# A fp32 Fourier/Hyena encoder layer: the weight parts of the first gate tiles are no longer held behind ScalarE's last row copy of the Fourier stage

## Chip, cores and metric
One core of a Trainium2 chip runs the whole program in one launch. The metric is device time in microseconds (us), the median of several runs. Two numbers of one profiled execution are used beside it: its own time, and the span that the profiler recorded. Engines are named as in the profile: PE (TensorE matmul), DVE (VectorE), ACT (ScalarE), POOL (GpSimd) and SP (the engine that issues most loads and stores).

## What is computed
Two sequences of 1024 rows and 1024 channels go through one encoder layer in float32. Cut to what matters here:

```
p = rmsnorm(x) @ w_in                      # fv, fg, hv (3 parts), hg, mg (2 parts)
fz = fftn(fv as 4 groups of 256, axes=(sequence, channel)).real
y_f = (fz * silu(fg)) @ w_fourier_out      # Fourier branch
kf = rfft(two implicit filters per channel, each normalised by its sum of magnitudes)
z = v; z = x1 * long_conv(z, kf[0]); z = x2 * long_conv(z, kf[1])   # Hyena branch
y_h = (z * silu(hg)) @ w_hyena_out
out = (sigmoid(mg_f) * y_f + sigmoid(mg_h) * y_h) @ w_out;  x + rmsnorm(out)
```

## The kernel before
**Numbers.** Every float32 operand is split into a high part h and a rest l, and a product is three matmuls (h·h, l·h, h·l), all recorded by one helper (L194). A split is a ScalarE copy to h (L171) and a DVE subtraction for l (L181).

**Stages.** `_body` (L1487) runs the set-up, `phase_fourier` (L489), `phase_main` (L901) and `phase_blocks` (the output projections). There is one instruction list for the whole program. Tile pools carry the buffers and their waits, and a scheduler that runs its own simulation of the engines' timelines when the program is built chooses in which order each engine gets its instructions; the order of the Python code is only its starting point. Within an engine that order is fixed: an instruction that waits holds everything behind it. `issue_after(ins)` puts in one more rule for that scheduler: what is made under it must stand behind `ins` on its engine.

**Fourier stage.** `fourier_half` (L386) runs four times, twice for each sequence. Near its end, for each of two channel groups g, it makes the odd part of the sequence transform (`pse`, `pso`, from tiles `oo`), turns it into `qp`, and for two column parts n multiplies by the channel tables into `pP` and `pQ`. ScalarE copies `pP` out twice (L475 into `fPs`, L476 scaled into `fPm`); DVE combines them with `pQ` into rows `fA` and `fB` (L480 to L485), and POOL issues the two stores to `d_fz` (L486, L487). In the kernel before, the name `self.rows` keeps the instruction of L476 that was made last: the last row copy of the last half.

**Main stage.** `load_x` loads the normalised input as eight parts, each split into `xh` and `xl` (128x1024; SP load, ScalarE cast, DVE subtraction). Then come 16 filters. `filter_taps` (L619) builds one filter's taps: `pft` matmuls, exponentials `ex` on ScalarE, taps `T` and a sum of magnitudes on DVE, two small `pn` matmuls (L652, L653) and a reciprocal on DVE (L654), which occurs once a filter and so marks the 16 steps in a trace. `filter_spectrum` (L660) transforms the taps (`pXf` matmuls, DVE before and after). The taps of filter i+1 are made ahead of the spectrum of filter i, and with the last filter the first two convolutions' projections are made as well.

**Gate tiles.** To give PE work beside the filters, 30 gate tiles (8 each of sections 0, 5 and 6 of `w_in`, 6 of section 4) are spread evenly over the 16 filters: one or two behind each, the first filter gets one. A gate tile (`spill_gate`, L793) calls `inproj` (L739), which takes the 128x1024 weight tile in two halves. A half needs: a place for its h and l (`rooms`: tags wh/wl with two buffers, then one tile `whl` in either of two more pools, in turn), an SP load into `wr` (two buffers, L757), a ScalarE copy to h (L762), a ScalarE multiplication that writes -h into l (L763), and a POOL-issued DMA that adds the weight from memory onto l (L764). Then 24 matmuls follow; with both halves a tile has 48 matmuls of 512 columns, 24 into each of two `pin` outputs of one PSUM bank (tag mm has four banks). ScalarE copies them out (L802, or Silu at L806 with a DVE product by `fz`), and SP stores them.

**What the change touches.** While the tile of the first filter is made, `self.opening` is true, and L762 and L763 stand under `issue_after(self.rows.ins)`: both ScalarE steps of that tile come behind the last row copy. The second tile has no rule of its own, but its `wr` loads need the buffers that the first tile's copies read.

After the filters, `branches` runs the convolutions of both sequences with further projections beside them.

Of the kernel before, what the change touches and what calls it, by code (L numbers as in the profile page):

```python
# [12 lines left out]
AF = mybir.ActivationFunctionType  # L13
# [148 lines left out]
class K:  # L162
# [223 lines left out]
    def fourier_half(self, b, half, W, fo, px, pf, begun={}):  # L386

        nc = self.nc
        WE, WO = W

        def pair(shape, tag, bufs=1):
            return [pf.tile(shape, F32R, tag=f"{tag}{i}", name=f"{tag}{i}", bufs=bufs) for i in range(2)]
# [54 lines left out]
        vec = self.vec  # L447
# [6 lines left out]
        for g in range(2):  # L454
            Pp, Qp = PP[g], pair([P, 514], "qp")
            co = slice(P * g, P * g + P)
            stage(P, lambda m: (OO[0][:, m, co], OO[1][:, m, co]), 1, None, Qp, "XT"[g])
            A = pf.tile([P, 1026], F32, tag="fA", name="fA", bufs=1)
            B = pf.tile([P, 1026], F32, tag="fB", name="fB", bufs=1)
            gg = 2 * half + g  # L460
            for n in range(2):
                w = (258, 256)[n]
                ns = slice(258 * n, 258 * n + w)
                pr, qr = (Pp[0][:, ns], Pp[1][:, ns]), (Qp[0][:, ns], Qp[1][:, ns])
                pP = self.psum("X", 2, "pP")[:, :w]
                self.mm3(pP, (ch[:, 0, 0:P], ch[:, 1, 0:P]), pr, True, False)
                self.mm(pP, cx[:, 0, g, :], PX[:, ns], False, True)
                pQ = self.psum("X", 2, "pQ")[:, :w]
                self.mm3(pQ, (ch[:, 0, P:2 * P], ch[:, 1, P:2 * P]), qr, True, False)
                self.mm(pQ, ch[:, 0, 2 * P:3 * P], pr[0], False, False)  # L470
                self.mm(pQ, ch[:, 0, 2 * P:3 * P], pr[1], False, False)
                self.mm(pQ, cx[:, 1, g, :], PX[:, ns], False, True)
                Ps = pf.tile([P, 258], F32, tag="fPs", name="fPs", bufs=2)
                Pm = pf.tile([P, 258], F32, tag="fPm", name="fPm", bufs=1)
                nc.scalar.copy(Ps[:, :w], pP)  # L475
                self.rows = nc.scalar.activation(Pm[:, :w], pP, AF.Copy, scale=vec[:, 11:12])  # L476
                t0 = 258 * n
                w = (258, 255)[n]
                r = slice(0, w)
                self.stt("dve", A[:, t0:t0 + w], pQ[:, r], vec[:, 10:11], Ps[:, r])  # L480
                self.add("dve", B[:, t0:t0 + w], pQ[:, r], Pm[:, r])
                w = (258, 254)[n]
                r = slice(0, w)
                self.stt("dve", A[:, 1024 - t0:1024 - t0 - w:-1], pQ[:, r], vec[:, 11:12], Ps[:, r])
                self.stt("dve", B[:, 1024 - t0:1024 - t0 - w:-1], pQ[:, r], vec[:, 12:13], Pm[:, r])  # L485
            nc.gpsimd.dma_start(self.d_fz[b][2 * gg], A[:, 0:1024])  # L486
            nc.gpsimd.dma_start(self.d_fz[b][2 * gg + 1], B[:, 0:1024])  # L487
# [251 lines left out]
    def inproj(self, sec, mt, b=None, plain=False):  # L739

        nc, a = self.nc, self.a
        ps = [self.psum("mm", 4, f"pin{n}") for n in range(2)]
        for q in range(2):
            s = slice(512 * q, 512 * q + 512)
            src = a["w_in"][sec, mt][:, s]
            kept = self.d_w[sec - 1][mt] if b is not None else None
            if b or plain:
                h, l = [self.wp.tile([P, 512], F32R, tag=g, name=g, bufs=2) for g in ("wh", "wl")]
            else:
                h, l = self.rooms()  # L750
            if b:
                self.keep_parts()
                for t, k in zip((h, l), kept):
                    nc.sync.dma_start(t.bitcast(F32), k[:, s])
            else:
                r = self.wp.tile([P, 512], F32, tag="w", name="wr", bufs=2)
                nc.sync.dma_start(r, src)  # L757
                if plain:
                    self.split(h, l, r, "dve", "act")
                else:  # L760
                    with self.tc.issue_after(self.rows.ins) if self.opening else ExitStack():
                        nc.scalar.copy(h, r)  # L762
                        nc.scalar.mul(l, h, -1.0)  # L763
                    nc.gpsimd.dma_start(l, src, accum_op=ADD)  # L764
                    self.keep_parts()
                    if kept:
                        self.unsaved = [(t, k[:, s]) for t, k in zip((h, l), kept)]
            h, l = [t.rearrange("p (a b) -> p a b", a=4) for t in (h, l)]
            for n in range(2):
                for kk in range(4):  # L770
                    k = 4 * q + kk
                    s = slice(512 * n, 512 * n + 512)
                    self.mm3(ps[n], (h[:, kk], l[:, kk]), (self.xh[k][:, s], self.xl[k][:, s]), k == 0, k == 7)
        return ps
# [126 lines left out]
    def phase_main(self, nct=8, nb=NB, nf=16):  # L901
        tc, nc, a = self.tc, self.nc, self.a
        with ExitStack() as es:
            pool = lambda n: es.enter_context(tc.tile_pool(name=n, bufs=1, reuse_waits="tile"))
            mf, wa, wb, mi = pool("mf"), pool("wa"), pool("wb"), pool("mi")
            self.stage2 = pool("m2")
            self.turn, self.unsaved = 3, []
            ws = Rooms(wa, wb)
            self.load_x(0, range(4))
            self.hid = ws.tile([P, L], F32R, tag="q", name="hid", bufs=2)  # L910
            hid = ws.tile([P, L], F32, tag="q", name="hidr", bufs=2)
            nc.sync.dma_start(hid, self.d_h)
            nc.scalar.copy(self.hid, hid)
            self.sub("dve", self.hid[64:128], hid[64:128], self.hid[64:128])
            taps = self.filter_taps(0, 0, ws)
            self.load_x(0, range(4, 8))
            self.cfw0 = mf.tile([P, 4 * P], F32, name="cfw0")
            self.cfwd = mf.tile([P, 2, 12 * P], F32R, name="cfwd")
            nc.sync.dma_start(self.cfw0, a["c_fw0"])
            nc.gpsimd.tensor_copy(self.cfwd[:, 0, 0:1], self.xl[4][:, 0:1])  # L920
            nc.gpsimd.dma_start(self.cfwd, a["c_fwd"])
            for t, n in ((self.th, "c_th"), (self.wsh, "w_short"), (self.bm, "b_merge")):
                nc.sync.dma_start(t, a[n])
            plain = [(5, c) for c in range(8)] + [(6, c) for c in range(8)] + [(4, c) for c in range(NH)]
            fill = sorted([((2 * c + 1) / len(plain), t) for c, t in enumerate(plain)]
                          + [((2 * c + 1) / max(NF, 1), (0, c)) for c in range(NF)])
            fill = [t for _, t in fill]
            for i in range(nf):
                nxt = self.filter_taps((i + 1) % 2, (i + 1) // 2, ws) if i + 1 < nf else None
                if i == nf - 1:  # L930
                    first = [self.conv(1 + n, 0, ws, "vx"[n], 0, True) for n in range(2)]
                self.filter_spectrum(i % 2, i // 2, taps, ws)
                taps = nxt
                self.opening = i == 0
                for sec, c in fill[i * len(fill) // nf:(i + 1) * len(fill) // nf]:
                    self.spill_gate(0, sec, c, ws)
                if i == min(2, nf - 1):
                    self.cinv = mi.tile([P, 2, INVW], F32R, name="cinv")
                    nc.gpsimd.dma_start(self.cinv, a["c_inv"])
            self.branches(nb, nct, ws, *first)  # L940
# [575 lines left out]
```

## Time and profile before

| | us |
|---|---|
| median of 3 runs | 2438.34 (2437.77 to 2440.07) |
| profiled execution, its own time | 2444.92 |
| profiled execution, its span | 2443.1 |
| PE busy, share of span | 2371.6 (97%) |
| DVE busy | 1986.3 (81%) |
| ACT busy | 1177.0 (48%) |
| POOL busy | 449.3 (18%) |

The granted TensorE clock over the span is 0.99 of full speed. The profiled execution took 6.58 us more than the median of the runs. A start time in a timeline is counted in us from the span's start; "x3" means three instructions put together in one row, the duration then being that of all; what stands in square brackets is how long the engine had waited before the row, and for whom. A view by windows gives, for each stretch of time, its length, the busy time of each engine with its number of instructions, the clock that was granted to PE (1.00 is full), and what the DMA engines did.

### The profile page before, as it was taken

The page shows a single profiled execution, that of the slowest core. Times are in us where ns is not written, and L with a number is a line of the kernel's source. Part 1 is how long each engine was busy: PE and PEld are TensorE (multiplying, and loading weights), DVE is VectorE, ACT ScalarE, POOL GpSimd, SP SyncE. Part 2 cuts the span into 40 slices and gives each one's busy share as a digit, 9 for nine tenths or more (in the row PEclk, how much of TensorE's full clock was granted, in tenths as well). Part 3 has the DMA queues.
Part 4 walks back from the last instruction along what each step waited for, and adds up shares of the span by engine and source line. Part 5 has one row for each costly group of instructions (what it writes and reads, how often), then busy time and mean ns, then how long its engine had stood idle before and what let it go on. Part 6 is the DMA issues. An engine that isn't in the chain of part 4 may idle for free. (4 is left out here: it accounts for less than half of the span.)

```text
span 2443.1 us, 37244 instructions
## 1 busy us (share of the span) xinstructions
PE 2371.6 (97%) x13006; PEld 2058.6 (84%) x13006; DVE 1986.3 (81%) x3840; ACT 1177.0 (48%) x2220; POOL 449.3 (18%) x568
## 2 busy tenths in 40 slices
PE   5998899999999999999999999999999999999998
PEld 4987788888888888888888888888888888888786
DVE  7687777777776899899899999998667687778777
ACT  5545677776754444343332322333334375656543
POOL 1331111111122232321124444310000000101000
PEclk9998899999999999999999999999999999999999
DMA  8544876777777767665455666553646687978744
GB/s 319 171 160 173 239 198 193 202 203 198 214 213 236 203 201 203 190 180 167 172 181 181 217 208 214 190 172 135 215 147 216 213 306 248 279 263 228 224 155 155
DMA packets 262980, 499.65 MB, mean 205 GB/s; under 512 B 26550, under 2 KB 90263, under 8 KB 262408
## 3 DMA queue, kind: packets, MB, share of 16 engines
q1 hardware_dynamic: 220076, 380.53, 46.7%
q0 software_dynamic: 42528, 116.72, 18.3%
q8 instruction: 102, 1.67, 0.3%
q14 instruction: 86, 0.70, 0.1%
q10 hardware_dynamic: 188, 0.02, 0.0%
HBM read 333.59 MB, written 167.77 MB: 205 GB/s over the span
## 5 line engine op out<-in xcount | busy, mean ns | idle before, releaser
L194 PE MATMUL pin<-xh,wl 128*128 128x512 f32 x1024 | 401.7, 394 | 3.0 <-DMA wl<-in_w_in 2.4
L194 PE MATMUL pin<-xh,wh 128*128 128x512 f32 x1024 | 403.2, 394 | 0.9 <-ACT wh L762 0.9
L194 PE MATMUL pin<-xl,wh 128*128 128x512 f32 x1024 | 402.8, 393 | 0.0
L194 PE MATMUL pin<-xh,whl 128*128 128x512 f32 x896 | 292.4, 396 | 0.0
L194 PEld LDWEIGHTS pin<-xh,wl 128*128 128x128 f32 x1024 | 193.8, 189 | 38.8 <-DMA wl<-in_w_in 2.6
L194 PEld LDWEIGHTS pin<-xh,wh 128*128 128x128 f32 x1024 | 194.0, 190 | 36.1 <-ACT wh L762 1.2
L194 PEld LDWEIGHTS pin<-xl,wh 128*128 128x128 f32 x1024 | 193.9, 189 | 35.0
L194 PEld LDWEIGHTS pin<-xh,whl 128*128 128x128 f32 x896 | 167.7, 189 | 32.5
L194 PE MATMUL pT<-cinv,yh 128*128 128x256 f32 x1024 | 192.8, 283 | 2.3 <-ACT yh L171 2.3
L194 PE MATMUL pin<-xl,whl 128*128 128x512 f32 x448 | 177.7, 397 | 0.0
L194 PEld LDWEIGHTS pT<-cinv,yh 128*128 128x128 f32 x1024 | 165.5, 191 | 12.4 <-ACT yh L171 2.7
L194 PE MATMUL pX<-bh,cfwd 128*128 128x256 f32 x768 | 159.5, 288 | 1.1 <-ACT bh L171 1.1
L181 DVE TENSOR_TENSOR t<-pX,k 128x1024 f32<-128x1024 f32 x128 | 156.1, 1219 | 4.0 <-PE pX L194 3.1
L171 ACT CAST yh<-y 128x512 fp32r<-128x512 f32 x128 | 79.3, 620 | 158.1 <-DVE y L181 120.4
L194 PE MATMUL pT<-cinv,yl 128*128 128x256 f32 x512 | 145.6, 284 | 0.0
L171 ACT CAST bh<-b 128x512 fp32r<-128x512 f32 x144 | 88.9, 619 | 105.9 <-DVE b L181 69.6
L194 PEld LDWEIGHTS pX<-bh,cfwd 128*128 128x128 f32 x768 | 126.1, 192 | 4.8 <-ACT bh L171 1.6
L181 POOL TENSOR_TENSOR draw<-draw 128x256 f32<-128x256 f32 x96 | 92.4, 963 | 114.8 <-DMA draw<-in_w_out 39.8
L181 DVE TENSOR_TENSOR bl<-b,bh 128x512 fp32r<-128x512 f32 x144 | 101.3, 706 | 12.0 <-ACT bh L171 11.9
L194 PE MATMUL pX<-bl,cfwd 128*128 128x256 f32 x384 | 109.7, 286 | 0.0
L181 DVE TENSOR_TENSOR yl<-y,yh 128x512 fp32r<-128x512 f32 x128 | 90.6, 708 | 16.4 <-ACT yh L171 16.2
L194 PEld LDWEIGHTS pT<-cinv,yl 128*128 128x128 f32 x512 | 98.2, 192 | 1.9
(366 smaller groups left out, 6091.9 us busy)
## 6 DMA issues: line engine op xcount, KB each, us to landing
k<-d_k SPq DMA_DIRECT2D x128, 512.0 KB, 4.4
wr<-in_w_in SPq DMA_DIRECT2D x136, 256.0 KB, 3.5
d_g<-gt SPq DMA_DIRECT2D x92, 256.0 KB, 3.5
d_k<-kt SPq DMA_DIRECT2D x128, 128.0 KB, 2.8
d_k<-kt SPq DMA_DIRECT2D x64, 256.0 KB, 2.5
fz<-d_g SPq DMA_DIRECT2D x64, 256.0 KB, 5.5
wl<-in_w_in POOLq DMA_DIRECT2D x56, 256.0 KB, 5.2
whl<-in_w_in POOLq DMA_DIRECT2D x56, 256.0 KB, 5.4
```

The lines of the kernel that those rows point to most:

```text
L171: self.rounded = nc.scalar.copy(h, src)
L181: return e.tensor_tensor(out, a, b, op=op)
L194: return self.nc.tensor.matmul(out, lhsT, rhs, start=start, stop=stop, skip_group_check=shared)
```

## The change
Three places are edited. The last row copy's instruction is no longer kept, the ScalarE steps of the first filter's gate tile no longer stand under `issue_after`, and the flag that told them apart is gone. The instructions themselves are the same; the scheduler is free to put them elsewhere. In the changed kernel line numbers from L762 on are lower by one, from L935 on by two.

```
@@ -473,7 +473,7 @@
                 Ps = pf.tile([P, 258], F32, tag="fPs", name="fPs", bufs=2)
                 Pm = pf.tile([P, 258], F32, tag="fPm", name="fPm", bufs=1)
                 nc.scalar.copy(Ps[:, :w], pP)
-                self.rows = nc.scalar.activation(Pm[:, :w], pP, AF.Copy, scale=vec[:, 11:12])
+                nc.scalar.activation(Pm[:, :w], pP, AF.Copy, scale=vec[:, 11:12])
                 t0 = 258 * n
                 w = (258, 255)[n]
                 r = slice(0, w)
@@ -758,9 +758,8 @@
                 if plain:
                     self.split(h, l, r, "dve", "act")
                 else:
-                    with self.tc.issue_after(self.rows.ins) if self.opening else ExitStack():
-                        nc.scalar.copy(h, r)
-                        nc.scalar.mul(l, h, -1.0)
+                    nc.scalar.copy(h, r)
+                    nc.scalar.mul(l, h, -1.0)
                     nc.gpsimd.dma_start(l, src, accum_op=ADD)
                     self.keep_parts()
                     if kept:
@@ -931,7 +930,6 @@
                     first = [self.conv(1 + n, 0, ws, "vx"[n], 0, True) for n in range(2)]
                 self.filter_spectrum(i % 2, i // 2, taps, ws)
                 taps = nxt
-                self.opening = i == 0
                 for sec, c in fill[i * len(fill) // nf:(i + 1) * len(fill) // nf]:
                     self.spill_gate(0, sec, c, ws)
                 if i == min(2, nf - 1):
```

The order of the built programs shows what moved. First ScalarE, before, around the last row copy (the L476 row; `wr`, `wh`, `wl`, `whl` are the weight half as loaded and its parts, `dec` and `ex` belong to the first filter's taps):

```order
L629 ACTIVATE dec<-dec 128x256
L640 ACTIVATE ex<-dec,vec 128x256 x2
L476 ACTIVATE fPm<-pP,vec 128x256
L762 CAST wh<-wr 128x512 x2
L640 ACTIVATE ex<-dec,vec 128x256 x2
L763 ACTIVATE wl<-wh 128x512 x2
L762 CAST whl<-wr 128x512 x2
L763 ACTIVATE whl<-whl 128x512 x2
```

ScalarE, changed, in the half before the last one, where the same eight steps now stand among that half's copies of `pse` into `qp` and of `pfv` into `oo`:

```order
L171 CAST qp_2237<-sst 128x514
L761 CAST wh<-wr 128x512
L475 COPY fPs<-pP 128x258
L476 ACTIVATE fPm<-pP,vec 128x258
L761 CAST wh<-wr 128x512
L762 ACTIVATE wl<-wh 128x512
L171 CAST oo_2487<-pfv_2614 128x256
L762 ACTIVATE wl<-wh 128x512
L761 CAST whl<-wr 128x512
L762 ACTIVATE whl<-whl 128x512
L761 CAST whl<-wr 128x512
L475 COPY fPs<-pP 128x256
```

All four weight halves (`wh` and `wl` hold the first tile's two, `whl` the second's) have moved up from the end of the last half of the Fourier stage into the half before it. On SP the loads of the second and third tile (`wr`, six of them in a row where two stood ahead of the load `hidr`) moved up with them, and on POOL the four accumulating DMAs now stand ahead of that earlier half's stores to `d_fz`.

PE, before, at the end of the last half of the Fourier stage (some 50 rows behind the half's last transforms): the last channel products `pQ`, and only then the first gate matmuls (`pin`; `xh_0` and `xl_0` are the first x part):

```order
L194 MATMUL pQ<-qp_2871,chan 128x256
L194 MATMUL pQ<-qp_2872,chan 128x256
L194 MATMUL pQ<-qp_2871,chan 128x256
L194 MATMUL pQ<-pp_2755,chan 128x256
L194 MATMUL pQ<-pp_2756,chan 128x256
L194 MATMUL pQ<-px,chx 128x256
L194 MATMUL pin_3301<-xh_0_2965,wh 128x512
L194 MATMUL pin_3301<-xl_0_2966,wh 128x512
L194 MATMUL pin_3302<-xh_0_2965,wh 128x512
L194 MATMUL pin_3302<-xl_0_2966,wh 128x512
L652 MATMUL pn<-acc,ones 128x128
```

PE, changed, at the first of that half's last transforms (`pse` from the tiles `oo`; `pin_3301` and `pin_3302` are the first tile's two outputs, `pin_3580` and `pin_3581` the second's):

```order
L194 MATMUL pin_3301<-xh_0_2965,wh 128x512
L194 MATMUL pin_3302<-xh_0_2965,wh 128x512
L194 MATMUL pin_3580<-xh_0_2965,whl 128x512
L194 MATMUL pin_3581<-xh_0_2965,whl 128x512
L194 MATMUL pse<-seq,oo_2487 128x258 x2
L194 MATMUL pse<-seq,oo_2488 128x258
L194 MATMUL pse<-seq,oo_2487 128x258 x2
L194 MATMUL pse<-seq,oo_2488 128x258
L194 MATMUL pin_3301<-xl_0_2966,wh 128x512
L194 MATMUL pin_3301<-xh_0_2965,wl 128x512
```

The gate matmuls now stand between the last transforms of the Fourier stage. Ahead of the first `pn` there are 177 of them instead of 4. The gate tiles run about four tiles earlier from there on (1413 `pin` instead of 1230 stand ahead of the 14th `pn`), and the list of gate tiles is used up sooner. Between the 14th and the 16th `pn` there stand 80 `pin` matmuls and 93 others where there were 195 and 116.

PE, changed, at the 15th `pn`: no `pin` matmul between the end of the first convolution projection (some 40 rows ahead) and `pin_8484`, the next projection (`b` and `bh`/`bl` are the filter's data, `cfw` and `cfwd` tables):

```order
L194 MATMUL pXf<-bh,cfwd 128x256 x2
L194 MATMUL pXf<-bl,cfwd 128x256
L194 MATMUL pXf<-bh,cfwd 128x256
L652 MATMUL pn<-acc,ones 128x128
L653 MATMUL pn<-ones,acc 128x2
L194 MATMUL pft<-w3s,hid 128x256 x14
L194 MATMUL pin_8484<-xh_0_2965,wh 128x512
L194 MATMUL pin_8484<-xl_0_2966,wh 128x512
```

More of the change, by code (lines that the diff above doesn't have):

```diff
@@ L475, in fourier_half @@
                 nc.scalar.copy(Ps[:, :w], pP)
-                self.rows = nc.scalar.activation(Pm[:, :w], pP, AF.Copy, scale=vec[:, 11:12])
+                nc.scalar.activation(Pm[:, :w], pP, AF.Copy, scale=vec[:, 11:12])
                 t0 = 258 * n
@@ L760, in inproj @@
                 else:
-                    with self.tc.issue_after(self.rows.ins) if self.opening else ExitStack():
-                        nc.scalar.copy(h, r)
-                        nc.scalar.mul(l, h, -1.0)
+                    nc.scalar.copy(h, r)
+                    nc.scalar.mul(l, h, -1.0)
                     nc.gpsimd.dma_start(l, src, accum_op=ADD)
@@ L933, in phase_main @@
                 taps = nxt
-                self.opening = i == 0
                 for sec, c in fill[i * len(fill) // nf:(i + 1) * len(fill) // nf]:
```

## The prediction
> **What bounds the kernel now.** I read the page's shares first, then the clock slices, then windows around the place of the change, then the timelines of the engines inside them.
>
> ```profile
> PE 2371.6 (97%) x13006; PEld 2058.6 (84%) x13006; DVE 1986.3 (81%) x3840; ACT 1177.0 (48%) x2220; POOL 449.3 (18%) x568
> PEclk9998899999999999999999999999999999999999
> ```
>
> PE is busy for 97% of the span, so an edit pays only where PE idles or runs at a lower clock. The second row, 40 slices of 61 us, shows the lower clock in the fourth and fifth slice, 183 to 305 us: the end of the Fourier stage. The windows there, from the last transforms of the last half to the second filter:
>
> ```profile
> core 0: us, PE busy (x) PEld busy (x) DVE busy (x) ACT busy (x) POOL busy (x), PEclk, DMA share, GB/s
> 224.30:253.80 29.50, 18.52 (x86) 15.70 (x85) 25.35 (x53) 20.57 (x43) 2.83 (x6) 0.67 0.54 199
> 253.80:270.20 16.40, 13.64 (x43) 10.64 (x42) 11.47 (x27) 7.02 (x16) 4.15 (x5) 0.66 1.02 303
> 282.90:641.90 359.00, 359.00 (x1952) 310.92 (x1951) 274.15 (x705) 256.82 (x561) 41.95 (x48) 1.00 0.73 200
> 641.90:701.60 59.70, 59.70 (x324) 51.59 (x324) 45.86 (x118) 38.50 (x87) 11.90 (x17) 1.00 0.80 226
> 720.00:740.00 20.00, 20.00 (x108) 17.22 (x107) 8.98 (x28) 10.86 (x23) 4.25 (x8) 1.00 0.97 290
> ```
>
> In the first two stretches, 45.90 us together, PE is idle for 10.98 + 2.76 = 13.74 us, and the rest runs at a granted clock of 0.67. DVE is the busy engine of the first (25.35 of 29.50). From 282.90 on PE is never idle and the clock is 1.00: through the filters, through the last two of them (641.90 to 701.60) and in the convolutions behind them (720 to 740). There, less or more work for another engine is worth nothing as long as PE has work queued.
>
> Why PE has no gate tile in the first stretch, in ScalarE's and PE's timelines (a row's last part is the idle time before it, and what ended it):
>
> ```profile
> 250.94 0.45 ACT L476 ACTIVATE fPm<-pP,vec 128x256 f32<-128x256 f32 x1
> 251.30 1.13 ACT L762 CAST wh<-wr 128x512 fp32r<-128x512 f32 x2
> 251.96 0.80 PE L194 MATMUL pin<-xh,wh 128*128 128x512 f32 x1 [0.92 <-ACT wh L762]
> 254.06 1.83 POOL L764 DMA_DIRECT2D wl<-in_w_in  x2 [0.43 <-ACT wl L763]
> 262.22 0.80 PE L194 MATMUL pin<-xh,wl 128*128 128x512 f32 x1 [2.37 <-DMA wl<-in_w_in]
> ```
>
> The last row copy begins at 250.94, the first weight cast follows it at once, and the first `pin` matmul waits for that cast. The rest part `wl` comes later still: PE waits again, 2.37 us, until the accumulating DMA has landed.
>
> **Part one: the front, gained.** The eight ScalarE steps, four SP loads (the second and third tile's) and four POOL-issued DMAs are moved, not added, so their own cost is nought; what counts is what they collide with where they stand now, at about 198 to 205 us:
>
> ```profile
> 197.85 0.62 ACT L171 CAST qp<-sst 128x514 fp32r<-128x514 f32 x1
> 201.39 0.37 ACT L475 COPY fPs<-pP 128x256 f32<-128x256 f32 x1 [2.01 <-PE pP L194]
> 205.59 0.62 ACT L171 CAST qp<-sst 128x514 fp32r<-128x514 f32 x1 [2.25 <-PE pQ L194]
> 193.74 1.21 SPq L757 DMA_DIRECT2D wr<-in_w_in  x2
> 209.40 0.33 SPq L912 DMA_DIRECT2D hidr<-d_h  x1
> 207.46 0.57 POOL L486 DMA_DIRECT2D d_fz<-fA  x1 [19.97 <-DVE fA L177]
> wr<-in_w_in SPq DMA_DIRECT2D x136, 256.0 KB, 3.5
> wl<-in_w_in POOLq DMA_DIRECT2D x56, 256.0 KB, 5.2
> ```
>
> ScalarE: eight steps of 1.13 / 2 = 0.57 us are 4.5 us. It waits 2.01 and 2.25 us in this stretch anyway, so some 4.3 of them lie in waits. The second pair of loads follows the first pair's casts; with 3.5 us from issue to landing it is there by about 203, just ahead of the casts that need it. Queued behind these on ScalarE is the `qp` cast of 205.59: a load that lands late delays it by 1 to 2 us, which I take as covered by the 2.25 us. SP: four more loads pass ahead of `hidr` (209.40), which the taps need; each waits for the cast two before it, the last one for the fourth cast, near 205, so they cost nothing unless the casts run late by over 4 us. POOL: the four DMAs pass ahead of the store of `fA`, before which POOL waited for 19.97 us; they cost nothing unless the last weight step ends after about 206. That store frees the buffer for DVE's next rows; late by d, it delays DVE by at most d.
>
> What PE gains. At full clock one 512-column matmul takes 0.23 us and one of 256 columns 0.72 / 6 = 0.12 us, from the starts of neighbouring rows:
>
> ```profile
> 271.37 0.39 PE L194 MATMUL pin<-xh,wh 128*128 128x512 f32 x1
> 271.60 0.39 PE L194 MATMUL pin<-xl,wh 128*128 128x512 f32 x1
> 224.26 0.88 PE L194 MATMUL pse<-seq,oo 128*128 128x258 f32 x6
> 224.98 0.88 PE L194 MATMUL pso<-seq,oo 128*128 128x258 f32 x6
> ```
>
> The 45.90 us hold 86 + 43 = 129 matmuls, and of these `pin` has
>
> ```profile
> 224.30:270.20 45.90, 12.13 (x30) 8.46 (x30) 0.00 (x0) 0.00 (x0) 0.67 0.71 236
> ```
>
> 30. So 30 x 0.23 + 99 x 0.12 = 6.9 + 11.9 = 18.8 us of work at full clock: 45.9 - 18.8 = **27.1 us** are lost there, to idling and the low clock. The changed order puts 177 `pin` ahead of the first `pn` where 4 stood, or 173 x 0.23 = 39.8 us more work, more than the hole. What must be there for them is the x parts, whose splits on DVE run at
>
> ```profile
> 221.91 1.23 DVE L181 TENSOR_TENSOR xl<-xl,xh 128x1024 fp32r<-128x1024 f32 x1
> 234.91 1.22 DVE L181 TENSOR_TENSOR xl<-xl,xh 128x1024 fp32r<-128x1024 f32 x1
> ```
>
> first and last. Part by part that is one every 1.9 us, and each serves 12 matmuls of the two tiles, 2.8 us, so PE is not starved by them. Where the stretch ends, DVE's chain is no longer hidden by PE's but stands beside it: 25.35 + 11.47 = 36.8 us of DVE work in 45.9, which fits. I take one wait as long as the 2.37 us of above as the price of the new interleaving: 27.1 - 2.4 = **24.7 us gained**. Bounds: 27.1 with no wait, 20 with three (7.1).
>
> **Part two: the tail, given back.** The list of 30 gate tiles has no more work than before, so what is done in the hole is missing later. The last two filters end with these reciprocals (14th, 15th, 16th):
>
> ```profile
> 642.28 0.17 DVE L654 RECIPROCAL invn<-pn 128x1 f32<-128x1 f32 x1 [0.34 <-PE pn L653]
> 671.65 0.17 DVE L654 RECIPROCAL invn<-pn 128x1 f32<-128x1 f32 x1 [1.92 <-PE pn L653]
> 702.13 0.17 DVE L654 RECIPROCAL invn<-pn 128x1 f32<-128x1 f32 x1 [3.18 <-PE pn L653]
> ```
>
> Between the 14th and 16th `pn`, before has 195 `pin` and 116 others: 195 x 0.23 + 116 x 0.12 = 58.8 us, against 59.70 measured, so these two prices reproduce the window within 1.5%. The changed order has 80 and 93 there: 18.4 + 11.2 = 29.6, by the same 1.5% **30.0 us**. PE no longer sets the pace of these two filters; DVE does, with 45.86 us of its own work, an order that differs little. The nearest row for a stretch that DVE paces with short PE pieces is the first window above: 25.35 of 29.50, or 0.86. That gives 45.86 / 0.86 = **53.4 us**, and 53.4 - 30.0 = **23.4 us given back**. Bounds: 45.9 (DVE never waits; 15.9 given back) and 59.7 (as long as before; 29.7).
>
> The low clock is in that 0.86, since it comes from a stretch granted 0.67. What makes PE lose its clock, in two-microsecond windows and PE's timeline:
>
> ```profile
> 218.00:220.00 2.00, 0.08 (x1) 0.00 (x0) 1.00 (x3) 1.62 (x5) 0.00 (x0) 1.00 0.94 338
> 222.00:224.00 2.00, 2.00 (x11) 1.66 (x10) 1.90 (x3) 1.67 (x3) 0.00 (x0) 0.50 0.93 309
> 224.00:226.00 2.00, 2.00 (x19) 1.98 (x18) 2.00 (x5) 1.29 (x3) 0.00 (x0) 1.00 1.03 422
> 220.13 0.51 PE L194 MATMUL pse<-alt,x5t 128*128 128x258 f32 x2 [2.05 <-DVE x5t L181]
> 240.31 0.63 PE L194 MATMUL pQ<-qp,chan 128*128 128x256 f32 x2
> 240.74 0.63 PE L194 MATMUL pQ<-pp,chan 128*128 128x256 f32 x2
> ```
>
> One idle time of 2.05 us, and within two microseconds the clock is at 0.50, though PE is busy; it is back at 224. At 0.50 a 256-column matmul takes 0.43 / 2 = 0.215 us. So I expect the tail's `pXf` and `pft` runs, which stand behind waits for DVE, at half clock. [...]
>
> **Between and behind.** In the 12 filters between, PE is busy all the time on both sides, with the gate tiles only about four earlier (183 `pin` at the 14th `pn`): nothing. Behind the 16th `pn` the convolutions' stretch leaves DVE and ScalarE half free (8.98 and 10.86 of 20.00): nothing.
>
> **Sum.** -24.7 + 23.4 = -1.3 us: the profiled execution would go from 2444.92 to 2443.6. It lies 6.58 above the median of the runs, 2438.34; so the median goes to **2437.0**. About 0.2%, 4.9 us, is what can be told from no change here: this is no change.
>
> **Rivals.** *Slower: the tail stays as long as before.* PE in the tail has each filter's `pft`, DVE's taps, the spectrum's `pXf` and DVE again in a row; with only 27 `pin` ahead of the 15th `pn`, nothing covers the time in which the engines wait for each other. If DVE waits 13.8 of 59.7 us, the tail costs 29.7 and the sum is -24.7 + 29.7 = +5.0: 2443.3; with 20 us gained at the front +9.7: 2448.0. It decides from a tail of 24.7 + 30.0 + 4.9 = 59.6 us. For it: three idle times of about 2 us in the first window, though ScalarE and DVE were the busy ones there. Against it: the scheduler can put the next filter's taps beside this one's spectrum, as its order at the 15th `pn` does. 0.20.
>
> *Faster: the tail keeps its full clock.* If the gaps in the tail stay too short to lower it, 49 `pXf` cost 0.12 instead of 0.215 us, 4.7 us less: a tail of 48.7, 18.7 given back, the sum -6.0: 2432.3. At DVE's floor of 45.9 with no wait at the front it would be -11.2: 2427.1. It decides below a tail of 49.8. [...] For it: 23 `pin` stand in a row ahead of the last spectrum. Against: the 2.05 us above. 0.30.
>
> *The hole is not filled.* The `pin` matmuls stand ahead of the last transforms in PE's queue; if they wait for x parts or for a late `wl`, they hold those transforms and with them DVE's chain. Were only half of the 27.1 won, the tail's price stays, and the sum is -13.6 + 23.4 = +9.8: 2448.1. Against it: the x parts come early enough as worked out. 0.08.
>
> **How the numbers follow.** No change has the remaining 0.42. Faster 0.30, slower 0.20 + 0.08 = 0.28. The range goes from about the floor case (2428) to the slower cases (2448); it leaves out little beyond DVE without any wait, and a front gain below half.
>
> **What would show it.** Right: `wh` casts near 198 to 205 on ScalarE; `pin` at 225 in PE's timeline; a clock near 1.00 and hardly any idle PE from 224 to 270; the first reciprocal near 224.3 + 177 x 0.23 + 82 x 0.12 + 2.4 = 277 (82 being the first window's 86 without its four `pin`); the 14th near 642.28 + 183 x 0.23 x 1.015 - 24.7 = 660; PE idle and a clock below 1.00 between the 14th and the 16th; about 53 us between these two. Wrong: a PE wait of over 3 us for `wl` or x ahead of 240, a 14th reciprocal later than 665, or a tail shorter than 50 or longer than 60.

## The result and the profile after
Over 13 runs each the changed kernel took 2436.56 us (2432.47 to 2438.85) and the kernel before 2441.60 us (2436.80 to 2446.73); the ratio is 0.998, with a 95% interval of 0.9971 to 0.9989. By that ratio it is 4.9 us less, between 2.7 and 7.1: a small gain, at the edge of what can be told from no change. The profiled execution went from 2444.92 to 2438.85 us, its span from 2443.1 to 2437.1.

The page of the changed kernel, its PE row and clock slices:

```profile
PE 2369.4 (97%) x13006; PEld 2057.8 (84%) x13006; DVE 1994.6 (82%) x3840; ACT 1174.9 (48%) x2218; POOL 441.9 (18%) x568
PEclk9999999999979999999999999999999999999999
```

The two slices at 8 are gone, and a slice at 7 has come: the twelfth, 670 to 731 us. The loss moved from the end of the Fourier stage to the last filters. The windows of the changed kernel, with the columns of before:

```profile
224.30:253.80 29.50, 29.50 (x166) 25.64 (x165) 19.16 (x36) 21.66 (x38) 3.37 (x5) 1.00 0.81 267
253.80:270.20 16.40, 16.40 (x84) 13.94 (x83) 9.65 (x23) 10.60 (x25) 4.02 (x6) 1.00 0.70 191
277.04:659.00 381.96, 381.96 (x2071) 330.43 (x2071) 292.38 (x753) 266.96 (x593) 50.06 (x61) 1.00 0.75 209
659.00:714.00 55.00, 40.89 (x191) 34.71 (x190) 47.30 (x119) 31.82 (x72) 3.35 (x5) 0.75 0.38 112
```

In the 45.9 us of the front PE is never idle and at full clock, and issues 250 matmuls instead of 129. From the first filter to the 14th it is busy throughout, as before. In the tail it is idle for 14.11 of 55.00 us and granted 0.75. The bounds of those windows are the reciprocals (1st, 14th, 15th, 16th):

```profile
277.04 0.17 DVE L654 RECIPROCAL invn<-pn 128x1 f32<-128x1 f32 x1 [5.28 <-PE pn L653]
659.01 0.16 DVE L654 RECIPROCAL invn<-pn 128x1 f32<-128x1 f32 x1
683.32 0.17 DVE L654 RECIPROCAL invn<-pn 128x1 f32<-128x1 f32 x1 [0.97 <-PE pn L653]
713.99 0.16 DVE L654 RECIPROCAL invn<-pn 128x1 f32<-128x1 f32 x1
```

Up to the 14th `pn` the changed order has 183 `pin` more, 183 x 0.233 = 42.7 us of PE work: 642.28 + 42.7 - 659.01 = 26.0 us were gained by then. The tail took 55.0 us for work of 30.0 (80 `pin` and 93 others at the prices of the prediction and the 1.5%): 25.0 given back. At the 16th `pn` that leaves about 1 us, or 1.3 by the finer count of the table further down. What else is gained, 4.7 us of the profiled 6.0, lies behind it.

### The profile page after: what moved, and what is told of

Its sections match the earlier page's. It is cut to its first block, busy times and chain, and to the rows that moved or that the text cites. A ratio compares the mean times of both kernels' runs of the same rounds, so it can differ in the third digit from the quotient of the medians.

```text
span 2437.1 us, 37253 instructions
## 1 busy us (share of the span) xinstructions
PE 2369.4 (97%) x13006; PEld 2057.8 (84%) x13006; DVE 1994.6 (82%) x3840; ACT 1174.9 (48%) x2218; POOL 441.9 (18%) x568
## 5 line engine op out<-in xcount | busy, mean ns | idle before, releaser
L181 POOL TENSOR_TENSOR draw<-draw 128x256 f32<-128x256 f32 x96 | 100.4, 1046 | 114.5 <-DMA draw<-d_sh 41.4
L181 DVE TENSOR_TENSOR bl<-b,bh 128x512 fp32r<-128x512 f32 x144 | 102.3, 713 | 14.1 <-ACT bh L171 14.0
L181 DVE TENSOR_TENSOR yl<-y,yh 128x512 fp32r<-128x512 f32 x128 | 95.9, 749 | 10.5 <-ACT yh L171 10.3
```

The lines of the kernel that those rows point to most:

```text
L181: return e.tensor_tensor(out, a, b, op=op)
```

## The experiments
The question was whether front and tail are one trade (theory A: gate tiles fill the hole, and the tail pays because the 30 tiles run out), what the new wait ahead of the front is, and where the gain behind the 16th `pn` comes from.

**Only the first tile freed.** The rule is kept, but for the second tile alone:

```
for j in range(i * len(fill) // nf, (i + 1) * len(fill) // nf):
    sec, c = fill[j]
    self.opening = j == 1
```

> Only the first gate tile is freed; the second one's ScalarE steps stand behind the last row copy. By the order 52 pin matmuls stand ahead of the first pn (before 4, changed 177) and 210 between the 14th and 16th (195, 80). Theory A (the hole in the Fourier stage is worth what PE is given there, and the tail pays because the 30 gate tiles run out): front gain 48 x 0.23 = 11 us, tail full, PE idle there under 4 us, ratio to before about 0.9955. Theory B (the front gain of any freed tile is paid back in full somewhere behind, whatever the list holds): ratio 0.998 to 1.000, like the whole change.

Measured: ratio 0.9947 (0.9930 to 0.9963). Front and tail of this kernel:

```profile
647.20:709.30 62.10, 62.10 (x329) 53.34 (x330) 48.07 (x120) 38.52 (x85) 11.57 (x16) 1.00 0.72 200
224.30:270.20 45.90, 36.20 (x176) 29.85 (x174) 38.30 (x82) 29.27 (x61) 6.99 (x11) 0.85 0.76 252
```

The front still loses 9.70 us to idling and some more to a clock of 0.85, but the tail is full, 62.10 of 62.10. Less work brought forward gives a faster kernel, against theory B. That theory A's ratio came out as well is in part chance: counted as above, 642.28 + 45 x 0.233 - 647.23 = 5.5 us are gained by the 14th `pn`, not 11, and 5.6 by the 16th. About as much again is gained in the convolutions (5.6 us, and 4.3 in a second pair of profiles, by the table below), of which theory A says nothing. So the full tail holds as theory A has it; that the hole is worth all the work that PE is given there does not. Why one tile costs the tail nothing was not tested. It fits that 30 tiles have 30 x 48 = 1440 matmuls and that only 1425 `pin` stand ahead of the 16th `pn` in the kernel before (1485 here), so that some gate work was left over there.

**The first two tiles freed**, with `self.opening = j == 2` in the same place.

> The first two gate tiles are freed, the third one's ScalarE steps stand behind the last row copy. By the order 100 pin ahead of the first pn, 166 between the 14th and 16th. Theory A: front gain 96 x 0.23 = 22 us less about 2.4 for a wait, tail of about 55 us with 52 us of PE work in it, so 3 to 6 us given back: net -14 to -16, ratio about 0.994. Theory B: ratio 0.998, no better than the whole change.

Measured: 0.9969 (0.9960 to 0.9978): between one tile and all of them, but only half of what was expected.

```profile
656.90:716.30 59.40, 55.41 (x285) 46.99 (x286) 48.11 (x120) 37.09 (x82) 10.07 (x14) 0.94 0.61 168
224.30:270.20 45.90, 40.42 (x210) 34.35 (x211) 31.34 (x67) 30.52 (x57) 4.79 (x9) 0.93 0.59 216
```

The tail took 59.4 us, not 55, for 52 us of work: it grows with the PE work put into it, so 55 was no fixed length. The front fell short too: by the 14th `pn` 642.28 + 95 x 0.233 - 656.93 = 7.5 us are gained where 19.6 were expected, and the tail gives them back. The whole gain of this kernel lies behind the 16th `pn`. And the first `pQ` product of the last group waits 5.59 us, as in the changed kernel, against 2.47 with one tile: the new wait comes with the second tile.

**Two more tiles in the list.** `NH = 8` instead of 6 in the changed kernel.

> The changed kernel with 32 gate tiles in the list instead of 30 (the last two of section 4, otherwise made inside the convolutions). Theory A: 157 pin instead of 80 between the 14th and 16th pn, the tail as long as now, 55 us, but filled; what was done there is missing from the saturated convolutions: 77 x 0.23 = 17.7 us won against the changed kernel, ratio to before about 0.991. Theory B, and the theory that the tail is long for its low clock alone: ratio 0.997 to 0.999, since filling the tail wins nothing that isn't lost to the two more stores and loads.

Measured: 1.0017 (1.0006 to 1.0027). Both theories had this wrong. The tail, and then the convolutions between 900 and 1700 us, of this kernel:

```profile
663.40:725.50 62.10, 54.44 (x281) 46.22 (x280) 48.30 (x122) 37.65 (x82) 9.06 (x12) 0.92 0.61 164
900.00:1700.00 800.00, 785.47 (x4633) 695.25 (x4632) 754.52 (x1337) 269.12 (x477) 232.17 (x270) 0.99 0.59 186
```

and the same stretch of the convolutions in the changed kernel:

```profile
900.00:1700.00 800.00, 797.81 (x4751) 707.66 (x4751) 756.06 (x1335) 273.94 (x482) 225.08 (x270) 1.00 0.58 186
```

In the tail 7 us of the 17.7 are lost, since it grew to 62.1. The larger loss is in the convolutions: PE idles for 14.53 us instead of 2.19. Clock was lost with the waits as well: over the 20 us from 1360, with 3.15 us of idling, PE was granted 0.74, where the changed kernel has 1.00 throughout. DVE is busy for 754 to 756 of 800 there, and the two tiles were what PE did beside it. So "the convolutions are saturated" was true only with those tiles in them.

**The same two tiles in the kernel before** (`NH = 8`), where front and tail stay as they are.

> The kernel before with 32 gate tiles in the list: front and tail as before by the order (4 pin ahead of the first pn, 194 between the 14th and 16th), only two tiles' work (22 us of PE) moves out of the convolutions to ahead of them. If the two tiles made the changed kernel slower because the convolutions need them as PE work beside DVE (idle PE there rose from 2 to 15 us between 900 and 1700), it is slower here too: ratio 1.004 to 1.006, idle PE in the convolutions about 20 us. If the loss came from the tail, it is the same here: 0.999 to 1.001.

Measured: 1.0109 (1.0096 to 1.0123).

```profile
900.00:1700.00 800.00, 778.26 (x4602) 689.51 (x4602) 743.73 (x1319) 268.13 (x471) 240.34 (x275) 0.99 0.60 186
```

PE idles for 21.74 us in the convolutions, as expected, against 6.23 in the kernel before; the time lost is twice as much as expected. A part of the rest is clock: what the granted clock lacks of full in each window of 20 us from 900 to 1780, times PE's busy time there, makes 9.7 us here and 3.2 before. The tail plays little part in it (the 16th reciprocal at 703.04, before 702.13; 2.3 us later per work done). The convolutions need those tiles.

**The tail alone.** The kernel before with `NH = 2`: four tiles fewer in the list, the front untouched.

> The kernel before, with four of section 4's gate tiles taken out of the list (26 instead of 30, those four made inside the convolutions): the first tile is held as before, so the front is unchanged, but the list runs out early: 73 pin between the 14th and 16th pn instead of 195, close to the 80 of the changed kernel. Theory A (an exhausted list costs the tail some 25 us, whatever the front does): tail about 55 us with 28 us of PE work in it, +27 us, ratio about 1.011, down to 1.007 if the four tiles take all of the 10 us of PE waits out of the convolutions. Rival (the tail is long in the changed kernel for another reason, and gate work can be moved behind it for nothing): ratio 0.998 to 1.002.

Measured: 1.0097 (1.0083 to 1.0111). The tail, between the 14th and the 16th reciprocal:

```profile
643.30:694.70 51.40, 36.05 (x176) 29.72 (x175) 46.54 (x117) 30.43 (x70) 2.73 (x4) 0.83 0.38 102
```

PE idles for 15.35 us and is granted 0.83, much like the tail of the changed kernel, though the first tile is held as before: an exhausted list alone makes this tail, 51.4 us for 28.2 of work, so 23.2 lost, and the median rose by 22.9.

**The hold moved up by part of a half.** The rule is kept, but `self.rows` is the second row copy of the half before the last:

```
row = nc.scalar.activation(Pm[:, :w], pP, AF.Copy, scale=vec[:, 11:12])
if (b, half, g, n) == (1, 1, 0, 1):
    self.rows = row
```

> The first tile's ScalarE steps stand behind a row copy as before the change, but behind the second of the half before the last one (about 207 us) instead of the last of all, so that the weights' POOL DMAs come behind the stores of fA and fB and not ahead of them. If the POOL DMAs of 201 to 205 us are what makes the fA/fB stores land late (DVE waits 3.66 and 1.92 us for them in the changed kernel, PE 5.54 us behind that, against 2.13 us before), the wait falls back to about 2 us and the time is 3 us below the changed kernel, ratio about 0.997. If the stores are late for another reason (the load traffic of SP), the wait stays and the ratio is 0.998.

Measured: 1.0013 (1.0003 to 1.0024), neither. POOL in this kernel, and PE's waits at the front and in the first convolution:

```profile
205.97 1.84 POOL L766 DMA_DIRECT2D wl<-in_w_in  x2 [17.69 <-ACT wl L765]
208.19 0.57 POOL L488 DMA_DIRECT2D d_fz<-fA  x1 [0.38 <-DVE fA L177]
209.81 1.83 POOL L766 DMA_DIRECT2D whl<-in_w_in  x2 [0.51 <-ACT whl L765]
...
219.46 1.01 PE L194 MATMUL pQ<-qp,chan 128*128 128x256 f32 x3 [6.61 <-DVE fB L177]
...
746.18 0.35 PE L194 MATMUL pXf<-bh,cfwd 128*128 128x256 f32 x1 [3.25 <-DVE kt L177]
```

The row copy came at 203.62 us, not at 207, so only two of the four DMAs stand behind the stores, and two still stand right ahead. The wait is longer, 6.61 us. With half as many ahead in the queue it did not shrink, but all the weights' transfers have come nearer to the stores as well, so this run does not tell the queue from the traffic. The first reciprocal comes 3.7 us later for it, the 16th 1.9, and a new wait of 3.25 us stands at the start of the convolutions.

**The stores on SP.** The changed kernel with `nc.sync` instead of `nc.gpsimd` for the two stores that land late.

> The changed kernel with the two stores of fA and fB that land late (issued at 207 and 208 us) issued by SP instead of POOL, so that they share no queue with the weights' accumulating DMAs. Up to the 16th pn the order of PE is that of the changed kernel; behind it the scheduler orders the convolutions otherwise. If POOL's queue makes them late: PE's wait of 5.54 us falls to 2 to 2.5, the first reciprocal comes 3 us earlier (274). If it is the traffic of all weights' transfers: the wait stays within a microsecond and the first reciprocal at 277. Whatever it is, if the order of the convolutions is worth several us by itself, the stretch from the 16th reciprocal to the last pin matmul, 1058.4 us in the changed kernel, differs by more than 2 us.

Measured: 0.9976 (0.9967 to 0.9985).

```profile
217.60 1.01 PE L194 MATMUL pQ<-qp,chan 128*128 128x256 f32 x3 [4.61 <-DVE fB L177]
```

The wait shrinks by 0.9 us only, and the first reciprocal is at 277.09: POOL's queue is not the main cause. On SP the stores stand behind weight loads, though, the last of them issued at 204.65, so that this run does not exclude a queue altogether. The traffic of the second tile's transfers as a whole fits: between 200 and 216 us the DMA engines' busy share is 0.39 before, 0.64 with one tile freed and 0.90 in the changed kernel. What part of it counts was not separated. The stretch from the 16th reciprocal to the last `pin` took 1058.6 us, against 1058.4: no effect of another order behind it.

**Both of them**, only the first tile freed and the stores on SP.

> Only the first tile freed, as in the first experiment, and the two stores on SP. Front as there (52 pin ahead of the first pn, wait of about 2.5 us, so nothing to win), 186 pin between the 14th and 16th pn instead of 210. Theory A: the tail still full; ratio 0.994 to 0.996, unless the other order of the convolutions moves it by up to 0.003.

Measured: 0.9984 (0.9975 to 0.9993), a miss. PE's wait for the stores fell to 0.98 us, but a longer one came behind it. ScalarE and PE in this kernel, and PE's clock behind the wait:

```profile
220.53 0.42 ACT L630 ACTIVATE dec<-dec 128x256 f32<-128x256 f32 x1 [2.43 <-DMA dec<-in_filt_decay]
224.73 0.80 PE L194 MATMUL pse<-alt,x5t 128*128 128x258 f32 x2 [4.59 <-DVE x5t L181]
225.00:229.00 4.00, 4.00 (x20) 3.54 (x21) 3.00 (x7) 3.11 (x5) 0.00 (x0) 0.50 1.03 422
```

and the same row of PE with one tile freed and POOL's stores:

```profile
222.72 0.51 PE L194 MATMUL pse<-alt,x5t 128*128 128x258 f32 x2 [0.80 <-DVE x5t L181]
```

The load of `dec` lands late, ScalarE makes `x5t` behind it, and PE waits 4.59 us and then runs at half clock. The first reciprocal is at 261.77 instead of 257.40, with the same 52 `pin` ahead of it. So the front lost time, where the expectation had seen nothing to win. At the 16th `pn` the kernel is 3.4 us later per work done (701.77, with 1438 `pin` ahead instead of 1485); the front accounts for that. The convolutions take 4.7 us more, and there the scheduler's other order, which the expectation allowed for, remains as a possible cause.

**The three kernels once more, on one chip.**

> The kernel before, unchanged, profiled once more, since a part of the gain of the changed kernel lies behind the 16th reciprocal: 1078.0 us from there to the last pin matmul before, 1058.4 after, of which 13.2 us are work that the changed kernel did ahead of it, which leaves 6.4 us. If these belong to the order of the convolutions' instructions, they are the same in another execution: about 1078 again, with PE idle for some 3.4 us between 900 and 1100. If they are one execution's chance, the stretch comes out several us shorter or longer.

> The changed kernel, unchanged, beside the two others on one chip. If the 6.4 us belong to the order: from the 16th reciprocal to the last pin again 1058 to 1059 us, ratio to before 0.9975 to 0.998. If they are chance: several us off.

> The first experiment's kernel (only the first tile freed) again, on the same chip as the changed kernel: if half the hole for no tail is the better trade, 0.994 to 0.996 and under the changed kernel's ratio by 0.002 to 0.004; if its first result was chance, both ratios agree within their intervals.

Measured: 2440.41 for the one run of the kernel before, 0.9981 (0.9971 to 0.9990) for the changed kernel, 0.9959 (0.9945 to 0.9972) with one tile freed. The order of the three holds, and the last is the fastest version found; the last two intervals just touch here, where those of the first measurement were apart.

The table puts the kernels on one scale. "Ahead" is the PE work that stands ahead of the 16th `pn` in excess of before, counted in the order of each kernel (a 512-column matmul at 0.233 us, shorter ones in proportion); it is taken off the 16th reciprocal's time and added to the stretch from there to the last `pin`.

| kernel | ahead, us | 16th reciprocal less ahead | convolutions plus ahead | ratio |
|---|---|---|---|---|
| before (and again) | 0 | 702.1 (701.8) | 1078.0 (1074.4) | 1 |
| changed (and again) | 13.2 | 700.8 (700.8) | 1071.6 (1071.9) | 0.998 (0.9981) |
| first tile freed (and again) | 12.8 | 696.5 (696.4) | 1072.4 (1070.1) | 0.9947 (0.9959) |
| two tiles freed | 14.1 | 702.2 | 1070.2 | 0.9969 |
| changed, 32 tiles | 36.1 | 689.4 | 1097.1 | 1.0017 |
| hold moved up | 11.9 | 704.0 | 1080.5 | 1.0013 |
| before, 26 tiles | -32.4 | 727.1 | 1077.5 | 1.0097 |
| before, 32 tiles | -1.4 | 704.4 | 1101.8 | 1.0109 |
| stores on SP | 13.2 | 701.0 | 1071.8 | 0.9976 |
| first tile freed, stores on SP | 1.9 | 699.9 | 1077.1 | 0.9984 |

Up to the 16th `pn` the change wins 1.0 to 1.3 us in both pairs of profiles. In the convolutions it wins 6.4 in the first pair and 2.5 in the second; the changed kernel's stretch is the same each time, and that of before differs by 3.6 between two executions. Where before loses it, in a window of before and the same one of the changed kernel:

```profile
900.00:1060.00 160.00, 156.58 (x928) 138.37 (x927) 146.49 (x269) 66.64 (x115) 46.76 (x58) 0.99 0.69 198
```

```profile
900.00:1060.00 160.00, 160.00 (x968) 142.46 (x968) 151.28 (x275) 68.61 (x117) 45.33 (x60) 1.00 0.69 202
```

Before idles for 3.42 us there (3.59 between 900 and 1100 in its second profile), the changed kernel not at all. So some 2.5 us go with the kernel. The rest goes with the execution, and it is clock: the longest of these waits is the same in both profiles of before, but only in the first was PE's clock lowered behind it. First profile, second profile:

```profile
1015.06 0.50 PE L194 MATMUL pT<-cinv,yh 128*128 128x256 f32 x2 [2.30 <-ACT yh L171]
1016.00:1020.00 4.00, 4.00 (x13) 3.10 (x12) 4.00 (x11) 1.66 (x4) 0.75 (x1) 0.59 0.91 269
```

```profile
1014.93 0.50 PE L194 MATMUL pT<-cinv,yh 128*128 128x256 f32 x2 [2.28 <-ACT yh L171]
1016.00:1020.00 4.00, 4.00 (x25) 3.55 (x24) 4.00 (x11) 1.75 (x4) 0.63 (x1) 1.00 0.88 268
```

Counted by windows of 20 us as above, the missing clock makes 3.2 us in the first profile and none in the second, nor in the changed kernel's two; the two stretches of before differ by 3.6. Why the changed order has no such wait was not settled: kernels with a like amount of work ahead fall on both sides (1072 and 1080).

## Why the prediction held, point by point
**The front.** The casts came at 198 to 204 us on ScalarE, the `qp` cast behind them at 205.58 (before 205.59): the waits did cover them. SP's load of `hidr` was issued at 209.41 (before 209.40). 24.7 us were forecast and 26.0 measured, and the first and 14th reciprocal, forecast near 277 and 660, came at 277.04 and 659.01. A wait of the kind that the prediction priced at 2.4 us, without knowing its place, did come, ahead of the stretch that it had counted. POOL, DVE and PE of the changed kernel show it, with the size of the two stores and the time from issue to landing:

```profile
204.54 0.86 POOL L763 DMA_DIRECT2D whl<-in_w_in  x1 [0.50 <-ACT oo L171]
207.45 0.57 POOL L486 DMA_DIRECT2D d_fz<-fA  x1 [2.05 <-DVE fA L177]
...
214.02 0.49 DVE L177 SCALAR_TENSOR_TENSOR fA<-pQ,vec,fPs 128x258 f32<-128x258 f32 x1 [3.66 <-DMA d_fz<-fA]
216.42 0.43 DVE L181 TENSOR_TENSOR fB<-pQ,fPm 128x258 f32<-128x258 f32 x1 [1.92 <-DMA d_fz<-fB]
...
217.69 1.01 PE L194 MATMUL pQ<-qp,chan 128*128 128x256 f32 x3 [5.54 <-DVE fB L177]
223.58 0.51 PE L194 MATMUL pse<-alt,x5t 128*128 128x258 f32 x2 [0.20 <-DVE x5t L181]
d_fz<-fA POOLq DMA_DIRECT2D x1, 512.0 KB, 6.4
d_fz<-fB POOLq DMA_DIRECT2D x1, 512.0 KB, 8.3
```

and the kernel before:

```profile
214.28 0.63 PE L194 MATMUL pQ<-qp,chan 128*128 128x256 f32 x3 [2.13 <-DVE fB L177]
d_fz<-fA POOLq DMA_DIRECT2D x1, 512.0 KB, 3.0
d_fz<-fB POOLq DMA_DIRECT2D x1, 512.0 KB, 4.9
```

The store of `fA` is issued when it was before, but lands 6.4 us after its issue instead of 3.0, and DVE may not write the next rows until then; PE waits 5.54 us where it waited 2.13, and `pse` starts 3.4 us later than the 220.13 of before. The sign of being wrong, a PE wait of over 3 us ahead of 240, had named `wl` and x and did not catch this one. The prediction had looked at the time at which the stores are issued; their landing is what counted.

**The tail.** 53.4 us were forecast from DVE's share of 0.86 in another stretch, 55.0 measured, and DVE's share in it is 47.30 / 55.00 = 0.86. That the two shares agree to two digits is luck: in the tail of the kernel before with 26 tiles, with nearly the same work, the share is 46.54 / 51.40 = 0.91, and with 52 us of PE work the tail was 59.4 long.

**The clock.** PE in the tail of the changed kernel, in three windows, and its longer waits:

```profile
668.00:670.00 2.00, 1.39 (x8) 1.00 (x7) 2.00 (x11) 1.90 (x6) 0.86 (x1) 0.87 0.20 70
670.00:684.00 14.00, 10.19 (x46) 9.46 (x46) 10.29 (x29) 9.02 (x23) 0.00 (x0) 0.53 0.41 118
684.00:700.00 16.00, 7.15 (x22) 5.38 (x22) 16.00 (x34) 7.02 (x15) 0.00 (x0) 0.58 0.18 57
```

```profile
667.08 0.50 PE L194 MATMUL pft<-w3s,hid 128*128 128x256 f32 x2 [0.84 <-DVE T L181]
669.14 0.39 PE L194 MATMUL pXf<-bh,cfwd 128*128 128x256 f32 x1 [0.50 <-ACT bh L171]
671.64 0.58 PE L194 MATMUL pXf<-bl,cfwd 128*128 128x256 f32 x1 [1.21 <-DVE bl L181]
677.18 0.55 PE L194 MATMUL pXf<-bh,cfwd 128*128 128x256 f32 x1 [2.40 <-ACT w3s L171]
688.25 1.22 PE L194 MATMUL pft<-w3s,hid 128*128 128x256 f32 x4 [2.10 <-DVE T L181]
695.22 0.80 PE L194 MATMUL pft<-w3s,hid 128*128 128x256 f32 x2 [5.75 <-DVE T L181]
```

The clock begins to fall before 670, behind waits of 0.84 and 0.50 us, and up to 684 no wait is longer than 2.40 us, yet the clock is at 0.53. The Trainium skill, "TensorE: Matmul & The Clock Gate", Part 1, puts the half rate behind an idle window of about 3.4 us. It also tells of a kernel whose PE idled briefly but often between groups of matmuls and lost its clock that way, without a length for these times. This tail agrees with the second and not with a limit of 3.4 us on a single gap. Nor is the length of one gap enough to go by, as the two profiles of before show (2.30 us with the clock lowered behind it, 2.28 without). The second rival fell on its own condition, that the gaps stay too short to lower the clock. In the first rival's terms the tail of 55.0 is below its 59.6. The third fell with PE busy for all of the front's 45.9 us.

**Behind the 16th `pn`.** This is the term that was mis-sized. The forecast was nothing, for PE was taken as busy and DVE as half free from one window, 720 to 740. Over most of the convolutions, in the kernel before,

```profile
900.00:1700.00 800.00, 793.77 (x4714) 704.47 (x4713) 744.69 (x1322) 272.49 (x481) 229.74 (x273) 1.00 0.59 186
```

DVE is busy for 744.69 of 800 us and PE idles for 6.23; 4.7 us came from behind the 16th `pn` in the first pair of profiles and 3.2 in the second (4.2 us between the spans, 1.0 of it up to there). So -1.3 became -4.9, 2.7 to 7.1, by the runs: the direction and the trade were right, and the rest is a part of the program that the change was not thought to reach.

**Luck.** The forecast median, 2437.0, and the measured one, 2436.56, lie close together by two errors that cancel. The forecast counted from 2438.34, the median of the first three runs, and 13 runs give 2441.60, 3.3 us more; the gain was 3.6 us larger than forecast.

## What to carry over
Where PE is busy nearly everywhere, filler work brought forward into a hole is missing from where it stood: count the work that is left at the far end, and bring forward only as much as is left over there. One tile freed, 11 us of work, won more than twice as much as the whole change, 173 matmuls or 40 us of work: 5.6 us against 1.3 by the 16th `pn`, with a gain in the convolutions that both have. Judge a stage by a window over all of it, since 20 us with a free DVE say nothing about the 1000 around them. And moved transfers are judged by when their neighbours land, not by when they are issued.

## What was not expected of the hardware
Two stores of 0.5 MB each, issued at the same time as before the change, took 6.4 and 8.3 us to land instead of 3.0 and 4.9, with four accumulating DMAs and four loads of 256 KB each, 2 MB more, begun within the 8.5 us ahead of them; issued by SP instead of POOL, the wait behind them was only 0.9 us shorter. The same PE wait of 2.3 us was followed by a clock of 0.59 in one execution of the kernel before and by a full clock in another. And the median of the kernel before was 2438.34 us over its first three runs and 2441.60 over all 13, a difference larger than the sum of the forecast, 1.3 us.
